# Hybrid decoder layer on one core: order of the differential norm, the dilated sum, the gate chunks and the MLP's first products

## The chip, the core and the metric

One NeuronCore of a Trainium2 chip runs the whole layer in one launch. It has five engines with a queue each: TensorE (PE; matmuls and transposes, its weight loads counted as PEld), VectorE (DVE), ScalarE (ACT), GpSimd (POOL) and SyncE (SP), which issues most DMA transfers; ScalarE issues the others. The metric is device time of one execution in microseconds (us), lower is better.

## The reference

Input x is 1024 tokens by 1024 channels, float32. What is computed, cut to what matters here:

```python
h = rms_norm(x, mix_norm_g)
proj = h @ w_in                       # q, k, v of four mixers, gate logits (4 x 1024 wide)
o_a = stick_breaking(...)             # 4 heads of 64
o_b = dilated(...)                    # 3 groups x 4 heads, windows 128/512/2048, dilation 1/4/16
                                      #   out = sum_g softmax_g(lse_g) * out_g
o_c = forgetting(...)                 # 4 heads
o_d = differential(...)               # 4 heads, softmax minus lam * softmax
o_d = rms_norm(o_d, diff_g) * diff_out_scale        # per head, over its 64 channels
branch = einsum('bsnc,ncd->bsnd', [o_a, o_b, o_c, o_d], w_branch)
gates = sigmoid(gate_logit)
x = x + sum_n(gates * branch) @ w_out
h = rms_norm(x, mlp_norm_g)
x = x + square(relu(h @ w_up)) @ w_down             # 4096 wide
return rms_norm(x, final_norm_g)
```

## The kernel before

All products are float32 in three matmuls: each operand is split into a high part (ScalarE or POOL copies it) and a low part (VectorE or POOL subtracts), and `mm3` (lines 150 to 152) adds high x high, high x low and low x high in PSUM. Weights come in pieces of 128x512 through the tags "wr" (raw, from SP), "wh" and "wl" (split), four buffers each.

Nobody writes out the order on each engine. The program is traced in the order of the Python text; a planner then simulates a timeline, takes at each moment the earliest traced instruction of an engine that is ready, and gives out the buffers of a tag as they come free. Lower work is thus pulled forward into gaps that the plan sees. On the chip each engine then runs its list strictly in that order.

Stages:

1. Norm of x and transposition to hTh, hTl (lines 214 to 222).
2. Twelve attention units (lines 831 to 866), two head pairs each of: differential (units 0, 1), dilated group 0 (2, 3), 1 (4, 5), 2 (6, 7), forgetting (8, 9), stick-breaking (10, 11). The loop attends unit i, makes `N_BEFORE[i]` gate chunks, projects unit i+1, makes `N_AFTER[i]` gate chunks. A gate chunk (`gate_ahead`) computes 128 gate logits of one branch for all 1024 tokens, 48 matmuls of 512 columns named lg, and stores them in DRAM (gl). They fill TensorE while attention waits for other engines; 26 of the 32 chunks are made here. `attend_diff` ends with the norm of the differential branch (lines 656 to 678): per half of the tokens, squares, a matmul with a block of ones (rms), logarithm and exponential on ScalarE, a correction step and the product on VectorE. After unit 9 come `dil_weights` and `dil_combine` (lines 732 to 781), which load the three dilated outputs and their weights (dow), multiply on POOL, add on VectorE and store ys. Score rows and norm scratch share the five buffers of tag "s"; q and k tiles the twelve of tag "qk".
3. Gating: for branches 3, 2, 1, 0 and eight column blocks dm, `gate` loads stored logits (sg<-gl) or computes those that are left (pg), `branch` multiplies by w_branch (pb), by the gate on VectorE (line 930), and adds to the merged sum (lines 933, 935) on VectorE or POOL. For the last branch the sum is split into mh and ml (lines 936, 937), the operands of the output projection `out_proj` (po), which adds to x1 (line 979).
4. `norm2` for the eight token blocks t (lines 1034 to 1063): scale (xn, line 1041), transpose (nt), split into the MLP's operands. The MLP's products are made in seven-product (Strassen-Winograd) form; blocks 4 to 7 feed differences called t1, t2, b22, and in place in raw t3 and t4.
5. MLP up: sixteen pairs of 128 columns (`up_pair`, products p1 to p7, matmuls named pu); the first two pairs run together. MLP down with the final norm behind it (pd).

Of the kernel before, what the change touches and what calls it, by code (L numbers as in the profile page):

```python
# [2 lines left out]

# [18 lines left out]
P = 128  # L22
T = 1024
# [19 lines left out]
N_BEFORE = (1, 4, 3, 3, 0, 0, 0, 0, 0, 1, 1, 0)  # L43
N_AFTER = (0, 1, 1, 0, 0, 0, 0, 0, 1, 0, 3, 3)
N_MID = (0, 4)
# [4 lines left out]

DW_AT = 2

UORDER = (0, 1, 2, 3, 4, 5)
# [8 lines left out]
def kernel(  # L62
# [128 lines left out]

    ys_d = [[dram.tile([P, T], F32, name=f"ys_{n}_{p}") for p in range(2)] for n in range(4)]
    dil_d = [[dram.tile([P, T], F32, name=f"dil_{g}_{p}") for p in range(2)] for g in range(3)]
    st_d = [dram.tile([2, 4, T], F32, name=f"st_{g}") for g in range(3)]
# [11 lines left out]
    with ExitStack() as actx:  # L206
# [282 lines left out]
        ahead = [(n, dm) for dm in (0, 2, 4, 6, 1, 3, 5, 7) for n in ORDER_N[1:]]  # L489
        ahead += [(ORDER_N[0], NK - 1), (ORDER_N[0], NK - 2)]  # L490

# [126 lines left out]
        def attend_diff(pr, qs, ks, vt):  # L618
            y = y_tile()
            for h in range(2):  # L620
                bias = ap_.tile([P, T], F32, tag="s", bufs=NS, name=nm("tb"))
                nc.vector.tensor_scalar_mul(bias, dist, DIF_SLOPES[2 * pr + h])
                for th in range(2):
                    o_ps = ps_o.tile([P, 512], F32, tag="o", name=nm("o"))
                    for qt in (2 * th, 2 * th + 1):
# [27 lines left out]
                        causal_pv(o_ps, vt, h, qt, rows)  # L653
                    o_evac(o_ps, y, h, th, 1)

            for th in range(2):
                sl = slice(th * 512, th * 512 + 512)
                sq = s_tile("sq")[:, 0:512]
                sh = ap_.tile([P, 512], F32R, tag="ptile", bufs=NPT, name=nm("sh"))
                slo = ap_.tile([P, 512], F32R, tag="ptile", bufs=NPT, name=nm("slo"))  # L660
                nc.scalar.activation(sq, y[:, sl], AF.Square)
                nc.scalar.copy(sh, sq)
                nc.vector.tensor_sub(slo, sq, sh.bitcast(F32))
                ps = ps_t.tile([P, 512], F32, tag="t", name=nm("rms"))
                nc.tensor.matmul(ps, ones_blk, sh, start=True, stop=False)
                nc.tensor.matmul(ps, ones_blk, slo, start=False, stop=True)
                m_ = s_tile("m_")
                m, r0 = m_[:, 0:512], m_[:, 512:1024]
                nc.scalar.activation(m, ps, AF.Identity, bias=eps_col)
                nc.scalar.activation(r0, m, AF.Ln)  # L670
                nc.scalar.activation(r0, r0, AF.Exp, scale=-0.5)

                nc.vector.tensor_mul(m, m, r0)
                nc.vector.tensor_mul(m, m, r0)
                nc.vector.tensor_scalar(m, m, -0.5, 1.5, op0=ALU.mult, op1=ALU.add)
                nc.vector.tensor_mul(m, m, r0)
                nc.vector.scalar_tensor_tensor(y[:, sl], y[:, sl], dg_col, m, op0=ALU.mult, op1=ALU.mult)
            nc.scalar.dma_start(ys_d[3][pr], y)

# [83 lines left out]
        def dil_combine():  # L763

            for p in range(2):
                for th in range(2):
                    sl = slice(th * 512, th * 512 + 512)
                    acc = None
                    for g in range(3):
                        ow = s_tile("dow")  # L770
                        o, w = ow[:, 0:512], ow[:, 512:1024]
                        nc.sync.dma_start(o, dil_d[g][p][:, sl])
                        for h in range(2):
                            nc.sync.dma_start(w[64 * h:64 * h + 64],
                                              dw_d[g, 2 * p + h:2 * p + h + 1, sl].to_broadcast([64, 512]))
                        nc.gpsimd.tensor_mul(o, o, w)
                        if acc is None:
                            acc = o
                        else:
                            nc.vector.tensor_add(acc, acc, o)  # L780
# [75 lines left out]
        for i in range(len(units)):  # L856
            nxt()
            for _ in range(N_BEFORE[i]):
                gate_ahead(*ahead.pop(0))
            if i + 1 < len(units):  # L860
                nxt = units[i + 1]()
            for _ in range(N_AFTER[i]):
                gate_ahead(*ahead.pop(0))
            if i == max(len(units) - 1 - DW_AT, 2 * max(UORDER.index(g) for g in (1, 2, 3)) + 1):
                dil_weights()
                dil_combine()

# [12 lines left out]
    with tc.tile_pool(name="gate", bufs=1, reuse_waits="tile") as gp:  # L880
# [39 lines left out]
        def branch(n, dm, th, w, ys, sg):  # L920
# [9 lines left out]
            nc.vector.tensor_mul(sg, pb, sg)  # L930
            add = (nc.vector, nc.gpsimd)[dm % 2 if n == ORDER_N[-1] else th].tensor_add
            if n != ORDER_N[-1]:
# [55 lines left out]
        for c in range(3):  # L988
            ws = wcols(w_out, c * 256, 256, nc.vector)
            for b in range(2):  # L990
                out_proj(b, c, ws)
                for dm in [left.pop(0) for _ in range(min(len(left), (2, 1)[b] if c < 2 else 1))]:
                    if dm % 2 == 0:
                        w = w_br(n, dm)
                    branch(n, dm, 1, w, ys, sgs[dm])
        assert not left
        load_x1(1)
# [36 lines left out]
    def norm2(t):  # L1034
# [16 lines left out]
        if t >= NH:  # L1051
# [13 lines left out]

    steps = ((3, (0, 1), nc.vector), (0, (2, 3), nc.vector), (1, (2, 3), nc.vector), (2, (2,), nc.vector),
             (3, (2, 3), nc.vector), (2, (3,), nc.gpsimd))
    for c, bs, eng in steps:
        ws = wcols(w_out, c * 256, 256, eng)
        for b in bs:  # L1070
            out_proj(b, c, ws)
            if (b, c) in ((0, 3), (1, 3), (2, 3), (3, 2)):
                norm2(2 * b)
                norm2(2 * b + 1)


    def load_pair(j):

        res = {}
        for n, k0, c0 in (("a11", 0, 0), ("a12", NH, 0), ("a22", NH, P), ("a21", 0, P)):  # L1080
            src = w_up[k0 * P:(k0 + NH) * P, j * 256 + c0:j * 256 + c0 + P].rearrange("(k p) c -> p k c", p=P)
            if j == 0:
                q = wp.tile([P, 520], F32, tag="wr", bufs=NWR, name=nm("wr"))[:, :H]
            else:
                q = up_[j % 2].tile([P, H], F32, tag="wq", bufs=4, name=nm("wq"))
            nc.sync.dma_start(q.rearrange("p (a b) -> p a b", a=NH), src)
# [7 lines left out]

    q0 = load_pair(0)
    gm_c.close()
    sa_d = {}
    up_c = ctx.enter_context(ExitStack())
    upt = up_c.enter_context(tc.tile_pool(name="upt", bufs=1, reuse_waits="tile"))
    up_ = [None, upt]  # L1100
    q1 = load_pair(1)

    def up_pair(j, q, c1, c2):

        def ctile(n):
            p_ = up_[(c2 if n[0] == "o" else c1)]
            return p_.tile([P, H], F32, tag="c", bufs=8, name=nm(n))

        s1, s2 = (upt.tile([P, H], F32, tag="ws", bufs=4, name=nm("ws")) for _ in range(2))
        pss = {}  # L1110
# [72 lines left out]

    ab = [up_pair(0, q0, 1, 0), up_pair(1, q1, 1, 0)]
    for i in ("s", "p1", "p2", "p6", "p5", "t3", "p7", "p3", "t4", "p4"):
        if i[0] == "t":
            for t in range(NH):
                split(part(i, t), raw[t][:, "34".index(i[1])])
            if i == "t4":
                rw_c.close()  # L1190
                up_[0] = up_c.enter_context(tc.tile_pool(name="up", bufs=1, reuse_waits="tile"))
                q = load_pair(2)
        else:
            for p_ in ab:
                p_[i]()
    for p_ in ab:
        p_["end"]()
    for j in range(2, NPAIR):
# [4 lines left out]
        q = q2  # L1203
    up_c.close()
    h2a_c.close()
    m_ctx.close()
# [160 lines left out]
```

## Time and profile before

| | us |
|---|---|
| median of 3 runs | 1934.98 |
| lowest, highest | 1934.52, 1936.77 |
| the profiled execution's own time | 1935.1 |
| span of its trace | 1933.4 |
| PE busy | 1847.4 |
| DVE busy | 1092.3 |
| ACT busy | 840.0 |
| POOL busy | 798.3 |

The span runs from the first to the last instruction of one profiled execution; rows of the profile give times from its start. Rows by stretch give the length, then for each engine its busy time and number of instructions, the mean clock that TensorE was granted (1.00 is full), the share of the DMA engines that was busy and GB/s. A row by instruction gives line, engine, operation, output and inputs; in a bracket stands the engine's idle time before it and whose result ended that. Where only three durations stand, they are minimum, median and maximum in ns.

### The profile page before, as it was taken

The numbers are of one execution on the slowest core, as the hardware profiler recorded it, in microseconds if no ns is written. First come the engines' busy times: TensorE is split into PE (matmuls) and PEld (weight loads), VectorE is DVE, ScalarE is ACT, GpSimd is POOL, SyncE is SP. The second block draws the span as 40 slices with busy tenths as digits, with TensorE's granted clock in tenths as the row PEclk, the third lists the DMA queues.
The fourth block names the chain that finished last, engine by engine and source line by source line (L and its number), as shares of the span: only waits on it lengthen the run. The fifth ranks groups of instructions, "written<-read, shape, count | busy, mean of one in ns | idle before, by whom it ended". The sixth has DMA issues, their size and how long they took to land.

```text
span 1933.4 us, 27274 instructions
## 1 busy us (share of the span) xinstructions
PE 1847.4 (96%) x9635; PEld 1551.8 (80%) x9635; DVE 1092.3 (56%) x1896; ACT 840.0 (43%) x1723; POOL 798.3 (41%) x727
## 2 busy tenths in 40 slices
PE   7999999999999999999899989969999998999997
PEld 7888877888888889878777779958888887788885
DVE  5143464535444456556761686595444444959587
ACT  4133443445444344424541543544554543444354
POOL 4333244422222433462313562175565631617164
PEclk9999999999999999999999989989999999999999
DMA  4734113234242312272203764434444439665355
GB/s 148 165 92 126 50 49 88 60 88 138 61 143 56 88 56 68 55 214 70 73 18 110 254 200 139 156 109 154 162 146 150 146 109 365 210 187 175 113 175 185
DMA packets 210104, 249.08 MB, mean 129 GB/s; under 512 B 16944, under 2 KB 136112, under 8 KB 209968
## 3 DMA queue, kind: packets, MB, share of 16 engines
q1 hardware_dynamic: 172288, 172.72, 29.6%
q10 hardware_dynamic: 37680, 74.63, 11.6%
q8 instruction: 76, 1.25, 0.3%
q14 instruction: 60, 0.49, 0.1%
HBM read 170.58 MB, written 63.08 MB: 121 GB/s over the span
## 4 chain that ended last, share of the span: by engine, by line
PE 81%; DVE 7%; DMA 5%; POOL 3%; issue 2%; ACT 2%; SPq 0%; POOLq 0%; DVEq 0%; ACTq 0%
PE pu L1127 5%; PE pu L1126 5%; PE pu L1125 5%; PE lg L150 5%; PE lg L151 5%; PE lg L152 5%; PE pd L1269 4%; PE pd L1268 4%; PE lin L152 4%; PE lin L151 4%; PE pd L1267 4%; PE lin L150 4%; PE pt L422 3%; PE linv L151 2%; PE linv L150 2%; PE linv L152 2%
## 5 line engine op out<-in xcount | busy, mean ns | idle before, releaser
L129 POOL TENSOR_SCALAR wh<-wr 128x512 fp32r<-128x512 f32 (+1 forms) x156 | 106.3, 684 | 420.8 <-PE linv L152 144.3
L130 POOL TENSOR_TENSOR wl<-wr,wh 128x512 fp32r<-128x512 f32 (+1 forms) x160 | 223.1, 1399 | 9.1
L1267 PE MATMUL pd<-wh,sh 128*128 128x512 f32 x448 | 175.1, 396 | 5.4 <-ACT sh L1028 5.3
L1268 PE MATMUL pd<-wl,sh 128*128 128x512 f32 x448 | 175.3, 396 | 0.0
L1269 PE MATMUL pd<-wh,sl 128*128 128x512 f32 x448 | 168.1, 397 | 3.5 <-DVE sl L1029 3.5
L150 PE MATMUL lg<-hTh,wh 128*128 128x512 f32 x416 | 165.9, 399 | 2.6 <-ACT gs L486 2.6
L151 PE MATMUL lg<-hTl,wh 128*128 128x512 f32 x416 | 165.6, 398 | 0.0
L152 PE MATMUL lg<-hTh,wl 128*128 128x512 f32 x416 | 165.2, 397 | 0.0
L1029 DVE TENSOR_TENSOR sl<-sr,sh 128x512 fp32r<-128x512 f32 x112 | 111.8, 999 | 85.2 <-ACT sh L1028 85.1
L151 PE MATMUL lin<-hTl,wh 128*128 128x512 f32 x384 | 153.6, 400 | 0.0
L150 PE MATMUL lin<-hTh,wh 128*128 128x512 f32 x384 | 153.2, 399 | 0.0
L152 PE MATMUL lin<-hTh,wl 128*128 128x512 f32 x384 | 152.0, 399 | 0.0
L1028 ACT CAST sh<-sr 128x512 fp32r<-128x512 f32 x112 | 69.6, 622 | 161.6 <-PE pd L1268 139.4
L427 DVE TENSOR_TENSOR ptl<-pt,pth 128x512 fp32r<-128x512 f32 (+2 forms) x168 | 99.6, 605 | 66.8 <-ACT pth L426 65.6
L426 ACT CAST pth<-pt 128x512 fp32r<-128x512 f32 (+2 forms) x168 | 85.3, 524 | 113.4 <-PE pt L422 108.9
L150 PE MATMUL linv<-wh,hTh 128*128 128x256 f32 (+1 forms) x384 | 112.4, 295 | 1.8 <-POOL wh L129 1.7
L151 PE MATMUL linv<-wl,hTh 128*128 128x256 f32 (+1 forms) x384 | 112.0, 292 | 0.0
L152 PE MATMUL linv<-wh,hTl 128*128 128x256 f32 (+1 forms) x384 | 111.5, 291 | 0.0
L1267 PEld LDWEIGHTS pd<-wh,sh 128*128 128x128 f32 x448 | 84.3, 188 | 27.1 <-ACT sh L1028 7.1
L1269 PEld LDWEIGHTS pd<-wh,sl 128*128 128x128 f32 x448 | 84.5, 189 | 25.8 <-DVE sl L1029 6.4
L1268 PEld LDWEIGHTS pd<-wl,sh 128*128 128x128 f32 x448 | 84.5, 189 | 20.1 <-DVE wl L1029 0.2
L431 PE MATMUL o<-pth,v 128*128 128x256 f32 (+1 forms) x348 | 92.0, 276 | 8.9 <-DVE y L442 4.2
(349 smaller groups left out, 5110.4 us busy)
## 6 DMA issues: line engine op xcount, KB each, us to landing
wr<-in_w_in_dram SPq DMA_DIRECT2D x132, 256.0 KB
br<-in_w_down_dram SPq DMA_DIRECT2D x96, 256.0 KB
sr<-sa_s SPq DMA_DIRECT2D x64, 256.0 KB
wq<-in_w_up_dram SPq DMA_DIRECT2D x60, 256.0 KB
gl<-gs ACTq DMA_DIRECT2D x52, 256.0 KB
sg<-gl SPq DMA_DIRECT2D x52, 256.0 KB
sa_s<-o ACTq DMA_DIRECT2D x48, 256.0 KB
sr<-sa_a SPq DMA_DIRECT2D x48, 256.0 KB
```

The source lines that it names most:

```text
L129: nc.gpsimd.tensor_scalar(hi, raw, 1.0, 1.0, op0=ALU.mult, op1=ALU.mult)
L130: (eng or nc.gpsimd).tensor_sub(lo, raw, hi.bitcast(F32))
L150: nc.tensor.matmul(ps, ah, bh, start=(i == 0), stop=False, skip_group_check=True)
L151: nc.tensor.matmul(ps, ah, bl, start=False, stop=False, skip_group_check=True)
L152: nc.tensor.matmul(ps, al, bh, start=False, stop=(i == n - 1), skip_group_check=True)
L427: nc.vector.tensor_sub(lo[:, :n], ps[:, :n], hi[:, :n].bitcast(F32))
L1029: nc.vector.tensor_sub(o[1], i, o[0].bitcast(F32))
L1125: nc.tensor.matmul(ps, w_, bh[:, k], start=start and k == 0, stop=False, skip_group_check=True)
L1126: nc.tensor.matmul(ps, w_, bl[:, k], start=False, stop=False, skip_group_check=True)
L1267: nc.tensor.matmul(ps, sh[0][:, ts_], w[0], start=start and j == 0, stop=False, skip_group_check=True)
L1268: nc.tensor.matmul(ps, sh[0][:, ts_], w[1], start=False, stop=False, skip_group_check=True)
L1269: nc.tensor.matmul(ps, sh[1][:, ts_], w[0], start=False, stop=last and j == NPAIR - 1, skip_group_check=True)
```

## The change

Five edits:

- The differential norm leaves `attend_diff`. The raw output is stored in DRAM (yd), and a new `diff_norm(pr)` loads it back by halves, with its scratch in two tiles of tag "s", and stores each half. It is called after the projection that follows units 3 and 4.
- `dil_combine` moves from unit 9 to unit 11, behind its attention and ahead of the last gate chunks; its tiles take tag "qk" in place of "s". `dil_weights` stays.
- The last entry of `N_AFTER` goes from 3 to 6, so 29 chunks are made ahead and three are left for the gating stage.
- In the last branch all additions are on VectorE, and for each output product the branch products of the second half come ahead of it, the w_out pieces behind them.
- `norm2(6)` and `norm2(7)` move behind the first product p1 of the MLP's pairs 0 and 1; pair 0's weights load after `norm2(3)`. The buffers of the first two and of all odd pairs are slices of x1's memory in place of a pool of their own.

```diff
-N_AFTER = (0, 1, 1, 0, 0, 0, 0, 0, 1, 0, 3, 3)
+N_AFTER = (0, 1, 1, 0, 0, 0, 0, 0, 1, 0, 3, 6)
+NORM_AT = 3
...
-        ahead += [(ORDER_N[0], NK - 1), (ORDER_N[0], NK - 2)]
+        ahead += [(ORDER_N[0], dm) for dm in range(NK - 1, 2, -1)]
...
+            nc.scalar.dma_start(yd_d[pr], y)
+
+        def diff_norm(pr):
             for th in range(2):
                 sl = slice(th * 512, th * 512 + 512)
-                sq = s_tile("sq")[:, 0:512]
+                ysq, mr = s_tile("ysq"), s_tile("mr")
+                y, sq, m, r0 = ysq[:, 0:512], ysq[:, 512:1024], mr[:, 0:512], mr[:, 512:1024]
...
-                nc.scalar.activation(sq, y[:, sl], AF.Square)
+                nc.sync.dma_start(y, yd_d[pr][:, sl])
+                nc.scalar.activation(sq, y, AF.Square)
...
-            nc.scalar.dma_start(ys_d[3][pr], y)
+                nc.scalar.dma_start(ys_d[3][pr][:, sl], y)
...
-                        ow = s_tile("dow")
+                        ow = ap_.tile([P, T], F32, tag="qk", bufs=NQK, name=nm("dow"))
...
             if i + 1 < len(units):
                 nxt = units[i + 1]()
+            if i == len(units) - 1:
+                dil_combine()
             for _ in range(N_AFTER[i]):
                 gate_ahead(*ahead.pop(0))
+            if i in (NORM_AT, NORM_AT + 1):
+                diff_norm(i - NORM_AT)
             if i == max(len(units) - 1 - DW_AT, 2 * max(UORDER.index(g) for g in (1, 2, 3)) + 1):
                 dil_weights()
-                dil_combine()
...
-            add = (nc.vector, nc.gpsimd)[dm % 2 if n == ORDER_N[-1] else th].tensor_add
+            add = (nc.vector, nc.gpsimd)[0 if n == ORDER_N[-1] else th].tensor_add
...
         for c in range(3):
-            ws = wcols(w_out, c * 256, 256, nc.vector)
             for b in range(2):
-                out_proj(b, c, ws)
-                for dm in [left.pop(0) for _ in range(min(len(left), (2, 1)[b] if c < 2 else 1))]:
+                for dm in [left.pop(0) for _ in range(min(len(left), 1 if b else 2))]:
                     if dm % 2 == 0:
                         w = w_br(n, dm)
                     branch(n, dm, 1, w, ys, sgs[dm])
+                if b == 0:
+                    ws = wcols(w_out, c * 256, 256, nc.vector)
+                out_proj(b, c, ws)
...
-            if j == 0:
+            if j == 1:
                 q = wp.tile([P, 520], F32, tag="wr", bufs=NWR, name=nm("wr"))[:, :H]
+            elif j == 0 or j % 2:
+                q = next(slot_q)
             else:
-                q = up_[j % 2].tile([P, H], F32, tag="wq", bufs=4, name=nm("wq"))
+                q = up_.tile([P, H], F32, tag="wq", bufs=4, name=nm("wq"))
...
+    slots = [[s[:, i * H:(i + 1) * H] for i in range(8)] for s in sums_x1]
+    slot_q, slot_c, slot_s = cycle(slots[0][:4]), cycle(slots[0][4:] + slots[1][4:]), cycle(slots[1][:4])
...
     for c, bs, eng in steps:
         ws = wcols(w_out, c * 256, 256, eng)
         for b in bs:
             out_proj(b, c, ws)
-            if (b, c) in ((0, 3), (1, 3), (2, 3), (3, 2)):
+            if (b, c) in ((0, 3), (1, 3), (2, 3)):
                 norm2(2 * b)
                 norm2(2 * b + 1)
+                if b == 1:
+                    q0 = load_pair(0)
...
-            for p_ in ab:
+            for k, p_ in enumerate(ab):
                 p_[i]()
+                if i == "p1":
+                    norm2(NT - 2 + k)
```

More of the change, by code (lines that the diff above doesn't have):

```diff
@@ L2 @@
 from contextlib import ExitStack
+from itertools import cycle
 import numpy as np
@@ L192 @@
     ys_d = [[dram.tile([P, T], F32, name=f"ys_{n}_{p}") for p in range(2)] for n in range(4)]
+    yd_d = [dram.tile([P, T], F32, name=f"yd_{p}") for p in range(2)]
     dil_d = [[dram.tile([P, T], F32, name=f"dil_{g}_{p}") for p in range(2)] for g in range(3)]
@@ L666, in attend_diff @@
                 nc.tensor.matmul(ps, ones_blk, slo, start=False, stop=True)
-                m_ = s_tile("m_")
-                m, r0 = m_[:, 0:512], m_[:, 512:1024]
                 nc.scalar.activation(m, ps, AF.Identity, bias=eps_col)
@@ L676, in attend_diff @@
                 nc.vector.tensor_mul(m, m, r0)
-                nc.vector.scalar_tensor_tensor(y[:, sl], y[:, sl], dg_col, m, op0=ALU.mult, op1=ALU.mult)
-            nc.scalar.dma_start(ys_d[3][pr], y)
+                nc.vector.scalar_tensor_tensor(y, y, dg_col, m, op0=ALU.mult, op1=ALU.mult)
+                nc.scalar.dma_start(ys_d[3][pr][:, sl], y)
         def attend_dil(g, pr, q, k, kl, vt, mnl):
@@ L1063, in norm2 @@
             nc.gpsimd.tensor_sub(b21, b21, t2)
[L1066 to L1071, printed above, removed]
-            if (b, c) in ((0, 3), (1, 3), (2, 3), (3, 2)):
-                norm2(2 * b)
-                norm2(2 * b + 1)
     def load_pair(j):
@@ L1093, in wsplit @@
         return o
-    q0 = load_pair(0)
-    gm_c.close()
     sa_d = {}
[L1098 to L1101, printed above, removed]
+    slots = [[s[:, i * H:(i + 1) * H] for i in range(8)] for s in sums_x1]
+    slot_q, slot_c, slot_s = cycle(slots[0][:4]), cycle(slots[0][4:] + slots[1][4:]), cycle(slots[1][:4])
     def up_pair(j, q, c1, c2):
         def ctile(n):
-            p_ = up_[(c2 if n[0] == "o" else c1)]
-            return p_.tile([P, H], F32, tag="c", bufs=8, name=nm(n))
-        s1, s2 = (upt.tile([P, H], F32, tag="ws", bufs=4, name=nm("ws")) for _ in range(2))
+            if c2 if n[0] == "o" else c1:
+                return next(slot_c)
+            return up_.tile([P, H], F32, tag="c", bufs=8, name=nm(n))
+        s1, s2 = next(slot_s), next(slot_s)
         pss = {}
@@ L1181, in up_pair @@
         return {"s": sums, "p1": p1, "p6": p6, "p2": p2, "p5": p5, "p7": p7, "p3": p3, "p4": p4, "end": end}
-    ab = [up_pair(0, q0, 1, 0), up_pair(1, q1, 1, 0)]
+    steps = ((3, (0, 1), nc.vector), (0, (2, 3), nc.vector), (1, (2, 3), nc.vector), (2, (2,), nc.vector),
+             (3, (2, 3), nc.vector), (2, (3,), nc.gpsimd))
+    for c, bs, eng in steps:
+        ws = wcols(w_out, c * 256, 256, eng)
+        for b in bs:
+            out_proj(b, c, ws)
+            if (b, c) in ((0, 3), (1, 3), (2, 3)):
+                norm2(2 * b)
+                norm2(2 * b + 1)
+                if b == 1:
+                    q0 = load_pair(0)
+    ab = [up_pair(0, q0, 1, 0), up_pair(1, load_pair(1), 1, 0)]
     for i in ("s", "p1", "p2", "p6", "p5", "t3", "p7", "p3", "t4", "p4"):
@@ L1190 @@
                 rw_c.close()
-                up_[0] = up_c.enter_context(tc.tile_pool(name="up", bufs=1, reuse_waits="tile"))
+                up_c = ctx.enter_context(ExitStack())
+                up_ = up_c.enter_context(tc.tile_pool(name="up", bufs=1, reuse_waits="tile"))
                 q = load_pair(2)
         else:
-            for p_ in ab:
+            for k, p_ in enumerate(ab):
                 p_[i]()
+                if i == "p1":
+                    norm2(NT - 2 + k)
     for p_ in ab:
@@ L1204 @@
     up_c.close()
+    gm_c.close()
     h2a_c.close()
```

## The prediction

> **What bounds the kernel now.** I read the page's first part, then TensorE's list of waits, then the busy time of each engine in stretches cut at the stages that the change touches, then single instructions in time order.
>
> ```profile
> span 1933.4 us, 27274 instructions
> PE 1847.4 (96%) x9635; PEld 1551.8 (80%) x9635; DVE 1092.3 (56%) x1896; ACT 840.0 (43%) x1723; POOL 798.3 (41%) x727
> ```
>
> TensorE is busy for 96%. The change removes no matmul, so all it can win is in the 86.0 us in which TensorE has nothing (1933.4 - 1847.4), and in stretches at half clock.
>
> ```profile
> PE nt L1046 <- DVE xn L1041: 6.9, 4, 4.4
> PE po L152 <- DVE ml L937: 5.0, 2, 2.5
> PE sc L637 <- DVE mn L638: 4.4, 1, 4.4
> PE pu L1127 <- DVE wl L1029: 4.0, 2, 2.5
> PE rms L665 <- ACT sh L662: 1.2, 1, 1.2
> PE po L151 <- DVE wl L130: 0.5, 1, 0.5
> PE rms L666 <- DVE slo L663: 0.4, 1, 0.4
> ```
>
> Total, number and longest in us: many causes, none large; VectorE (DVE) ends most of them.
>
> ```profile
> core 0: us, PE busy (x) PEld busy (x) DVE busy (x) ACT busy (x) POOL busy (x), PEclk, DMA share, GB/s
> 225.00:258.00 33.00, 25.88 (x152) 22.46 (x151) 20.85 (x37) 17.38 (x32) 11.98 (x10) 0.90 0.15 41
> 398.00:430.00 32.00, 31.77 (x199) 28.17 (x199) 12.46 (x29) 17.67 (x32) 7.91 (x8) 1.00 0.31 88
> 430.00:475.00 45.00, 42.40 (x322) 39.24 (x320) 26.96 (x86) 27.56 (x83) 7.45 (x8) 1.00 0.31 97
> 855.00:876.00 21.00, 15.91 (x75) 11.74 (x73) 11.95 (x14) 7.89 (x17) 11.38 (x15) 1.00 0.74 196
> 876.00:945.00 69.00, 69.00 (x378) 57.75 (x378) 44.65 (x49) 31.98 (x69) 14.23 (x25) 1.00 0.17 54
> 945.00:990.00 45.00, 34.52 (x209) 28.02 (x209) 40.42 (x46) 29.92 (x65) 15.04 (x21) 0.96 0.18 53
> 1025.00:1075.00 50.00, 50.00 (x217) 40.40 (x216) 6.74 (x10) 5.58 (x10) 18.59 (x20) 1.00 0.25 73
> 1075.00:1110.00 35.00, 34.63 (x148) 27.41 (x147) 28.36 (x36) 22.31 (x38) 22.42 (x19) 1.00 0.93 319
> 1110.00:1148.00 38.00, 34.87 (x158) 27.77 (x157) 37.48 (x46) 19.76 (x34) 30.07 (x22) 1.00 0.70 223
> 1148.00:1164.00 16.00, 11.96 (x70) 11.66 (x71) 7.50 (x11) 2.88 (x7) 2.74 (x3) 0.68 0.29 102
> 1254.00:1300.00 46.00, 30.25 (x144) 23.50 (x143) 43.70 (x45) 21.45 (x43) 37.61 (x24) 0.81 0.38 121
> 1300.00:1590.00 290.00, 290.00 (x1251) 234.74 (x1250) 141.37 (x182) 144.82 (x238) 160.06 (x115) 1.00 0.43 144
> ```
>
> The idle of TensorE (length minus PE busy) sits in five places: 7.1 us at the first differential norm, 5.1 at the dilated sum, 10.5 where the gate chunks run out beside the last attention unit, 4.0 at the first output products, 15.8 at the last norms before the MLP. Where fillers are there (876 to 945, 1300 to 1590) it is 0. A 512-wide matmul costs 290/1251 = 0.232 us.
>
> **Part A, differential norm.** It leaves the end of attend_diff and comes after the projections of units 4 and 5, through DRAM: two 512 KB stores of y, four 256 KB loads on SP, four 256 KB stores instead of two of 512 KB. Arithmetic, matmuls and table loads are the same.
>
> ```profile
> 251.12 0.39 PE L637 MATMUL sc<-dm,dm 128*128 128x256 f32 x1 [4.38 <-DVE mn L638]
> L661 ACT ACTIVATE sq<-y x4: 616/618/620, 224.7 to 413.0; 128x512 f32<-128x512 f32 x4
> L670 ACT ACT_TABLE_LOAD  x4: 1283/1283/1283, 239.4 to 419.6; - x4
> L674 DVE TENSOR_TENSOR m__344_1425<-m__344_1425 x1: 1671/1671/1671, 244.7 to 244.7; 128x512 f32<-128x512 f32 x1
> ```
>
> At the first norm TensorE waits 1.2 + 0.4 for the rms operands, then 4.4 for unit 1's scores, whose L638 is queued on VectorE behind the norm's multiplies (L674 took 1.67). These 6.0 go. The clock is 0.90 over 33 us, 3.3 us lost; I count half as following the 4.4 wait: 1.7. Saved: 7.7. The second norm lies in 398 to 430, where TensorE idles only 0.2: nothing to win there.
>
> The new place: a half of a norm costs ScalarE five operations of 0.62 and two table loads of 1.28, 5.7 us, so 11.4 per norm on ScalarE, in a dilated stretch like 430 to 475, where it has 27.6 of 45 busy and TensorE already idles 2.6. Queued behind the norm there are L710's exponentials and the ptile casts, for which the transposes and P·V wait; the cover is the next unit's lin and linv matmuls. Bounds per norm: 0.2 (the second norm) to 7.7 (the first). The second is the nearer row, as fillers stand beside it; I take 2.1. A saves 7.7 - 4.2 = **3.5** (ends -7.7 and 7.3). The extra 2 MB find a DMA share of 0.31, and ten issues more on SP and ScalarE at about 0.4 each stand beside other work: nothing, unless SP waits for a slot of tag "s" with weights queued behind; that is inside the upper bound.
>
> **Part B, dilated sum out of 855 to 876.**
>
> ```profile
> 864.52 0.44 PE L403 MATMUL sc<-kA,qA 128*128 128x384 f32 x1 [2.99 <-ACT sg L513]
> 867.63 0.44 PE L422 MATMUL pt<-ident,sg 128*128 128x128 f32 x2 [1.22 <-DVE sg L517]
> L774 SPq DMA_DIRECT2D dow<-dw x24: 444/502/1113, 830.6 to 860.0; - x24
> L776 POOL TENSOR_TENSOR dow<-dow x12: 1263/1292/1751, 834.4 to 865.2; 128x512 f32<-128x512 f32 x12
> L780 DVE TENSOR_TENSOR dow<-dow,dow x8: 671/1267/1766, 838.3 to 867.5; 128x512 f32<-128x512 f32 x8
>   DMA dow<-dw: 14.1, 6
> ```
>
> The sg tiles of the stick-breaking unit share tag "s" with dow here. With dow in tag "qk" the waits of 2.99 and 1.22 go: **4.2** (0 to 5.1). Late next is the unit's own chain of VectorE scans.
>
> **Part C, three more chunks and the sum beside the last unit.** Three chunks are 3 x 48 x 0.232 = 33.4 us of matmuls, moved from 1025-1075 into the stretch that idles 10.5 us. There TensorE was 100% busy on them, so the gating stage gets shorter by 33.4 and the last unit longer by 33.4 - 10.5. With the clock (0.96 over 45 us, 1.7) that saves 12.2. Each chunk takes along two weight loads on SP, two splits on POOL, two ScalarE copies, two stores and two loads; a chunk already hidden in 876 to 945 shows the price, 0.
>
> Against it: the sum now stands there, before the six chunks in the program. Its 12 multiplies are 15.5 us of POOL, which also waits up to 14.1 for dow's transfers, and the kp memsets and weight splits queue behind them; its 24 issues of dw alone hold SP for 24 x 0.50 = 12.0 us with wr loads behind; its 8 adds are 10.1 us of VectorE, busy 40.4 of 45. TensorE still has 33.4 - 10.5 = 22.9 us of filler to cover the delay. Bounds: 0, to the 5.1 that the same sum cost at 855; I take half, 2.5. C saves **9.7** (7.1 to 12.2).
>
> **Part D, output products.**
>
> ```profile
> L930 DVE TENSOR_TENSOR sg<-pb,sg x48: 675/678/692, 1089.6 to 1200.2; 128x512 f32<-128x512 f32 x48
> L935 DVE TENSOR_TENSOR sg<-mg,sg x8: 676/686/693, 1137.7 to 1199.6; 128x512 f32<-128x512 f32 x8
> L935 POOL TENSOR_TENSOR sg<-mg,sg x8: 1585/1660/1674, 1138.0 to 1200.9; 128x512 f32<-128x512 f32 x8
> 1149.58 0.54 PE L152 MATMUL po<-wh,ml 128*128 128x256 f32 x1 [2.52 <-DVE ml L937]
> 1153.66 0.58 PE L152 MATMUL po<-wh,ml 128*128 128x256 f32 x1 [2.47 <-DVE ml L937]
> ```
>
> The first product waits twice for ml, at the end of the chain DVE L930, POOL L935, ACT mh, DVE ml. The change makes eight adds 0.69 on VectorE instead of 1.66 on POOL (VectorE +5.5 us, outside the saturated 1110-1148 for the most part) and puts two branch products, 2 x 12 x 0.232 = 5.6 us, ahead of the out_proj. The 5.0 go. In 1148-1164 the clock is 0.68, 5.1 us lost, 3.9 of it with work on TensorE (half of one 2.5 us wait taken off): also gone. New: w_out's splits now come after the branches' VectorE work, so po may wait for wl; between the 0.5 that stands in the list of waits and all 8.9 of the gain. I take 3.0, nearer to the row: **5.9** (0 to 8.4).
>
> The Trainium skill, TensorE: Matmul & The Clock Gate, section HAM oscillation, holds that the clock halves after idle gaps of more than about 3.4 us. By that rule the waits of 2.5 don't cause the slow stretch, D is 2.0 and the time 1911; the trace differs, since 2.52 is the longest gap ahead of it.
>
> **Part E, norms and MLP.** p1 of both first pairs now comes before norm2(6) and norm2(7), and pair 0's weights load earlier, into x1's old place.
>
> ```profile
> 1264.73 0.40 PE L1125 MATMUL pu<-b11h,wh 128*128 128x512 f32 x1
> 1286.39 0.80 PE L1127 MATMUL pu<-b11h,wl 128*128 128x512 f32 x1 [2.46 <-DVE wl L1029]
> 1294.83 0.50 PE L1126 MATMUL pu<-mh,wh 128*128 128x512 f32 x1 [1.86 <-DVE mh L1029]
> ```
>
> VectorE is the bound here: 43.7 of 46 us. The planner has already pulled pair 0's p1 to 1264.7; what can still move into the idle is pair 1's p1 and both p2, so that at 1294.8, when the last norm's t2 operand is ready, one product less remains: 12 x 0.232 = 2.8. Pair 0's three POOL sums can start earlier, which may take POOL's interference off a few VectorE operations; I take 1.7 for that and the clock. E saves **4.5** (0, as VectorE has the same work, to 8, half of the 15.8 idle).
>
> **Sum.** 3.5 + 4.2 + 9.7 + 5.9 + 4.5 = 27.8. The profiled execution took 1935.1 us with a span of 1933.4; the median shown is 1934.98, the same within 0.2. 1935.1 - 27.8 = 1907.3, so 1907 us.
>
> **Rivals.**
> - *Everything fills:* upper ends, 7.3 + 5.1 + 12.2 + 8.4 + 8 = 41: 1894 us. For it: idle 0 wherever fillers stand. Against: VectorE at 43.7 of 46.
> - *The stalls move along:* both norms cost 7.7 again and the sum 5.1: A -7.7, C 7.1, total 14.0, 1921 us. For it: ScalarE at 27.6 of 45 before the norm comes.
> - *VectorE holds D and E:* these give 0; 17.4, 1918 us. For it: 37.5 of 38 us in 1110-1148.
> - *Slower: the gating stage doesn't shrink.* If transfers and VectorE set its length, the 33.4 us are added beside attention and not taken off in 1025-1148: C is 9.7 - 33.4 = -23.7, total -5.6, 1941 us. It turns to slower once more than 27.8 of the 33.4 stay. For it: DMA share 0.93 and VectorE 37.5 of 38. Against: over these 123 us VectorE has 72.6, transfers 71.7, and TensorE would still have 119.5 - 33.4 = 86.1.
>
> **How the numbers follow.** Forecast (1899 to 1916) 0.46; everything fills 0.13; stalls move along 0.14; VectorE holds D and E 0.10; parts cancel to within 0.2% 0.08; slower 0.09. 0.2% (3.9 us) is about what a measurement can tell from no change here. Faster: 0.46 + 0.13 + 0.14 + 0.10 = 0.83. Range 1890 to 1931: it leaves out the slower rival, most of the cancelling and a little of the low end.
>
> **What the next profile would show.** A: no wait of 4 us for L638 near 250, no rms wait above 2 us beside the dilated units. B: no wait of sc for sg L513 near 865. C: lg until the end of the last unit, no idle row like 945-990, three pg chunks instead of six. D: no po wait for ml, clock 1.00 there. E: both p1 before the last eight transposes, less than 15 us idle, VectorE still above 90%. Wrong if POOL or SP, waiting for dow, starves the chunks, or if the planner, which orders all of this anew, opens waits in places that the change doesn't touch.

## The result and the profile after

The changed kernel takes 1905.97 us (median of 6 runs, 1904.28 to 1908.19) against 1936.03 us for the kernel before on the same chip (6 runs, 1934.52 to 1939.13): ratio 0.9843, 95% interval 0.9831 to 0.9856. The forecast was 1907 us. The profiled execution took 1908.19 us, the longest of the six, with a span of 1906.4.

The first part of the page of the changed kernel:

```profile
span 1906.4 us, 27323 instructions
PE 1840.0 (97%) x9635; PEld 1551.8 (81%) x9635; DVE 1089.6 (57%) x1904; ACT 847.3 (44%) x1731; POOL 789.8 (41%) x719
```

The span is 27.0 us shorter. TensorE has the same 9635 matmuls; its idle time fell from 86.0 to 66.4 us (1906.4 - 1840.0), which is 19.6, and its busy time by 7.4. The clock doesn't explain the latter: inside the stretches at half clock between 150 and 1650 us TensorE was busy for 33.9 us before and 36.4 us after. What does is not shown.

TensorE's list of waits in the changed kernel (total, number, longest in us):

```profile
PE nt L1057 <- DVE xn L1052: 5.9, 3, 3.2
PE rms L674 <- ACT sh L671: 5.8, 1, 5.8
PE po L155 <- DVE ml L947: 2.7, 2, 1.4
PE po L154 <- POOL wl L133: 2.7, 3, 1.7
PE pt L426 <- ACT s L717: 2.4, 1, 2.4
PE pu L1127 <- DVE wl L1040: 0.6, 1, 0.6
PE po L154 <- DVE wl L133: 0.6, 1, 0.6
```

The 4.4 for L638, the 4.0 of pu for wl (0.6 is left) and 2.3 of the 5.0 for ml are gone. The wait of rms for sh was 1.2 and is 5.8, and that of po for wl from POOL, 1.0 before, is 2.7.

Busy time by stretch in the changed kernel, in the columns of the rows before:

```profile
225.00:258.00 33.00, 30.88 (x191) 27.27 (x190) 18.91 (x53) 13.64 (x37) 15.36 (x17) 0.95 0.18 49
258.00:510.00 252.00, 251.84 (x1423) 217.79 (x1422) 121.01 (x307) 113.08 (x256) 86.42 (x88) 1.00 0.32 92
465.00:510.00 45.00, 45.00 (x253) 38.87 (x252) 22.49 (x56) 26.42 (x56) 13.86 (x14) 1.00 0.40 109
510.00:545.00 35.00, 25.48 (x169) 22.76 (x168) 19.09 (x53) 22.71 (x52) 0.00 (x0) 0.80 0.10 38
855.00:876.00 21.00, 21.00 (x120) 17.63 (x119) 13.54 (x17) 8.53 (x19) 8.91 (x9) 1.00 0.65 199
870.00:892.00 22.00, 17.13 (x77) 13.82 (x76) 11.68 (x13) 7.56 (x17) 15.28 (x13) 0.84 0.71 212
990.00:1048.00 58.00, 58.00 (x275) 47.70 (x274) 16.45 (x19) 13.43 (x25) 20.11 (x19) 1.00 0.40 128
1048.00:1092.00 44.00, 44.00 (x190) 35.51 (x189) 30.59 (x43) 26.22 (x45) 28.19 (x24) 1.00 0.91 310
1230.00:1275.00 45.00, 33.60 (x163) 26.22 (x162) 44.62 (x48) 23.97 (x47) 40.56 (x27) 0.85 0.35 115
```

The row for 258 to 510 reads as follows before the change:

```profile
258.00:510.00 252.00, 246.29 (x1342) 208.90 (x1341) 119.11 (x311) 108.81 (x248) 86.64 (x91) 1.00 0.29 83
```

The old idle at 855 to 876 and at the end of the last unit is filled, that at 225 to 258 fell from 7.1 to 2.1 us, and 5.7 us in small pieces between 258 and 510 fell to 0.2. The idle of 9.5 us in 510 to 545 and of 4.9 us in 870 to 892 is new. Before the MLP VectorE has 44.62 of 45 us and TensorE still lacks 11.4.

To place the saving I cut both traces at four events that both have: the first matmul of cum_ps in the forgetting units, the 288th matmul with w_branch (pb), the 720th of the output projection (po), the first of MLP down (pd). Length of each stage in us, with the leave-one-out kernels told of below:

| | to cum_ps | to 288th pb | to 720th po | to pd | rest |
|---|---|---|---|---|---|
| before | 656.2 | 476.2 | 121.9 | 347.0 | 332.1 |
| after | 653.3 | 460.5 | 117.4 | 342.5 | 332.7 |
| norm back (A undone) | 656.9 | 460.4 | 116.7 | 342.7 | 332.4 |
| sum back (B undone) | 652.1 | 465.9 | 117.5 | 342.9 | 333.0 |
| 3 chunks (C undone) | 650.4 | 472.8 | 116.8 | 343.1 | 332.2 |
| products as before (D undone) | 651.8 | 460.5 | 120.6 | 342.0 | 332.5 |
| norms and MLP as before (E undone) | 652.0 | 459.6 | 117.5 | 347.0 | 330.5 |

Each part moves the stage that it stands in; B and C share the second. There is one trace for each kernel. A stage that no edit touches repeats to within about 3 us in the first and last column and 1 us in the third and fourth, which is finer than the runs' times can tell. The 653.3 of the changed kernel is at the upper end of what its first stage takes with the norm as changed (650.4 to 653.5).

### The profile page after: what moved, and what is told of

Same layout as the page of the kernel before. It is cut to its first block, busy times and chain, and to the rows that moved or that the text cites. A ratio compares the mean times of both kernels' runs of the same rounds, so it can differ in the third digit from the quotient of the medians.

```text
span 1906.4 us, 27323 instructions
## 1 busy us (share of the span) xinstructions
PE 1840.0 (97%) x9635; PEld 1551.8 (81%) x9635; DVE 1089.6 (57%) x1904; ACT 847.3 (44%) x1731; POOL 789.8 (41%) x719
## 3 DMA queue, kind: packets, MB, share of 16 engines
q10 hardware_dynamic: 39120, 77.25, 12.2%
## 4 chain that ended last, share of the span: by engine, by line
PE 85%; DVE 5%; DMA 4%; POOL 2%; issue 1%; ACT 1%; SPq 0%; POOLq 0%; DVEq 0%; ACTq 0%
PE pu L1126 5%; PE pu L1127 5%; PE pu L1125 5%; PE lg L153 5%; PE lg L154 5%; PE lg L155 5%; PE lin L154 5%; PE lin L153 5%; PE lin L155 5%; PE pd L1286 4%; PE pd L1285 4%; PE pd L1284 4%; PE pt L426 3%; PE linv L153 2%; PE linv L154 2%; PE linv L155 2%
## 5 line engine op out<-in xcount | busy, mean ns | idle before, releaser
L154 PE MATMUL lg<-hTl,wh 128*128 128x512 f32 x464 | 185.9, 401 | 0.0
L153 PE MATMUL lg<-hTh,wh 128*128 128x512 f32 x464 | 185.3, 399 | 0.0
L155 PE MATMUL lg<-hTh,wl 128*128 128x512 f32 x464 | 185.0, 399 | 0.0
L153 PEld LDWEIGHTS lg<-hTh,wh 128*128 128x128 f32 x464 | 87.8, 189 | 17.6
L155 PEld LDWEIGHTS lg<-hTh,wl 128*128 128x128 f32 x464 | 87.8, 189 | 17.4
```

The lines of the kernel that those rows point to most:

```text
L153: nc.tensor.matmul(ps, ah, bh, start=(i == 0), stop=False, skip_group_check=True)
L154: nc.tensor.matmul(ps, ah, bl, start=False, stop=False, skip_group_check=True)
L155: nc.tensor.matmul(ps, al, bh, start=False, stop=(i == n - 1), skip_group_check=True)
```

## Experiments

Each diff is against the changed kernel. Its ratio is to the kernel before, run on the same chip.

**Each part undone alone.** Norm: `attend_diff` ends with the norm of before, and

```diff
-            if i in (NORM_AT, NORM_AT + 1):
-                diff_norm(i - NORM_AT)
```

> The changed kernel with the differential norm back at the end of attend_diff. Theory (each part fills its own gap, and the norm's new place costs a stall of its own near 530): about 3 us slower than the changed kernel, 1909 us; the 4.4 us wait for L638 near 250 comes back, the waits of 5.8 and 2.4 us near 530 go. Rival (the new stall eats the whole gain): within 1 us of the changed kernel, 1906. Second rival (forecast's size of 7.7 for the first norm, with a cheap new place): 1913.

Measured: 1910.70 us, 0.9865 (0.9848 to 0.9881). Some 4 us more than after by the ratios, in the first stage (3.6, with the spread of 3 just told). TensorE's waits at 230 to 260 us with the norm back:

```profile
PE sc L640 <- DVE mn L641: 4.4, 1, 4.4
PE rms L668 <- ACT sh L665: 1.2, 1, 1.2
```

They are the two of before to the tenth, so the first norm's waits were read rightly.

Sum:

```diff
-            if i == len(units) - 1:
-                dil_combine()
...
                 dil_weights()
+                dil_combine()
...
-                        ow = ap_.tile([P, T], F32, tag="qk", bufs=NQK, name=nm("dow"))
+                        ow = s_tile("dow")
```

> The changed kernel with the dilated sum back behind unit 9 and its tiles back in tag s. Theory of the forecast (sg tiles wait for slots of tag s that dow holds): 4 to 5 us slower, 1911, with a wait of sc for sg L517 near 860. Rival (the stall comes with the sum wherever it stands, since its store ys<-dow waits in ScalarE's queue for the addition, and it only moved from 864 to 883): within 1.5 us of the changed kernel, 1906.

Measured: 1912.82 us, 0.9875 (0.9860 to 0.9889); 5.4 us more in the second stage. The wait of sc for sg is back at 859.75 us with 2.38. ScalarE's list of waits from 850 to 880 us tells what sg waited for:

```profile
ACT sg L517 <- DMA ys<-dow: 2.2, 1, 2.2
```

Chunks:

```diff
-N_AFTER = (0, 1, 1, 0, 0, 0, 0, 0, 1, 0, 3, 6)
+N_AFTER = (0, 1, 1, 0, 0, 0, 0, 0, 1, 0, 3, 3)
...
-        ahead += [(ORDER_N[0], dm) for dm in range(NK - 1, 2, -1)]
+        ahead += [(ORDER_N[0], dm) for dm in range(NK - 1, NK - 3, -1)]
```

> The changed kernel with three chunks beside the last unit instead of six (26 ahead, six left for the gating stage). Theory (the chunks fill TensorE's idle time at the end of attention): 10 to 12 us slower, 1917, with some 10 us idle before the last scores. Rival (the sum, now standing there, already changes the end of attention, and the rest of B and C is not the chunks): less than 5 us slower, 1910.

Measured: 1918.75 us, 0.9903 (0.9887 to 0.9920); 12.3 us more in the second stage, the largest single part. The end of the last unit, with three chunks:

```profile
945.00:990.00 45.00, 38.79 (x205) 31.99 (x204) 31.44 (x34) 20.61 (x44) 13.46 (x16) 0.89 0.18 53
```

6.2 us of idle and a clock of 0.89 return there.

Output products: the loop and the alternating additions of before.

```diff
-            add = (nc.vector, nc.gpsimd)[0 if n == ORDER_N[-1] else th].tensor_add
+            add = (nc.vector, nc.gpsimd)[dm % 2 if n == ORDER_N[-1] else th].tensor_add
...
+            ws = wcols(w_out, c * 256, 256, nc.vector)
             for b in range(2):
-                for dm in [left.pop(0) for _ in range(min(len(left), 1 if b else 2))]:
+                out_proj(b, c, ws)
+                for dm in [left.pop(0) for _ in range(min(len(left), (2, 1)[b] if c < 2 else 1))]:
```

> The changed kernel with the order of branch and output products and the alternating additions of before. Theory (the shorter chain and one branch product more ahead of po take about half of the waits for ml): 2.7 us slower, 1908.7, two po waits of 2.5 us come back. Forecast's size: 5.9 us slower, 1912.

Measured: 1909.08 us, 0.9853 (0.9834 to 0.9873); by the times alone not told from the changed kernel, but its third stage is 3.2 us longer, and two waits of 2.5 and 2.7 us for ml are back (1125 to 1145 us):

```profile
PE po L155 <- DVE ml L947: 5.2, 2, 2.7
```

Norms and MLP: the order of steps, `norm2` calls and buffers of before.

```diff
-                if i == "p1":
-                    norm2(NT - 2 + k)
```

> The changed kernel with norm2(6), norm2(7) ahead of the MLP and the buffers of before. Theory (products that need no late norm fill TensorE while VectorE works through the norms): 6 us slower, 1912; idle of about 15 us in the stretch from the last out_proj to the p6 products instead of about 11. Rival (VectorE is the bound there and has the same work): within 1.5 us, 1906.

Measured: 1910.00 us, 0.9863 (0.9846 to 0.9879); the fourth stage is 347.0 us, as before. TensorE's waits from 1230 to 1275 us:

```profile
PE nt L1057 <- DVE xn L1052: 6.7, 3, 4.5
PE pu L1138 <- DVE wl L1040: 4.1, 2, 2.5
PE pu L1136 <- ACT wh L1039: 2.0, 1, 2.0
```

The waits of the MLP's first products return. In this kernel, as before the change, 12 matmuls of pu come ahead of the last sixteen transposes nt; in the changed one 48 do.

**The additions alone.** The branch additions alternate again, the new order of products stays (the first pair of lines of the diff for the output products).

> The last branch's additions alternate between VectorE and POOL again; the order of branch products and output products stays as changed. Theory (the order is what counts, since ml is made on VectorE and the change puts two branch products between the making of ml and its reading): within 1 us of the changed kernel, 1905 to 1908 us, and waits for ml of 1.4 us or less each. Rival (the additions on VectorE are what shortened ml's way: POOL takes 1.2 us or more for an addition that VectorE does faster): waits for ml of 2 us or more return and with them the 1.9 us that both halves are worth, 1908 to 1911 us.

Measured: 1911.10 us, 0.9864 (0.9851 to 0.9878); third stage 120.8 us, as long as with the whole part undone (120.6). TensorE's waits from 1125 to 1145 us:

```profile
PE po L155 <- DVE ml L947: 3.5, 3, 2.1
PE po L153 <- ACT mh L946: 0.8, 1, 0.8
```

So the theory falls and the rival holds: with the new order, what part D wins comes from the additions on VectorE; the new order alone wins nothing. The additions with the old order were not run.

**The dilated sum: tiles, queues, engines.** First only the tag: the sum at unit 9 again, its tiles still in "qk".

```diff
-            if i == len(units) - 1:
-                dil_combine()
...
                 dil_weights()
+                dil_combine()
```

> The changed kernel with the dilated sum back behind unit 9, but its tiles left in tag qk. Tells tag from place. Theory of the forecast (slots of tag s are what held up sg): like the changed kernel or a little faster, 1906, no sg wait near 860. Rival (ScalarE's queue, with the store ys<-dow in it): a stall of 4 to 5 us remains, as with the sum wholly back. If q and k tiles of unit 11 wait for the sum's tiles: slower still, 1912.

Measured: 1921.39 us, 0.9918 (0.9902 to 0.9935); the slowest of all. The second stage takes 472.9 us against 465.9 with tag "s" at the same place. TensorE's waits from 835 to 880 us:

```profile
PE pt L426 <- DVE sg L521: 7.7, 3, 4.2
PE o L437 <- DVE ptl L431: 3.2, 2, 2.0
```

Taking the sum out of the slots of tag "s" at the old place makes it worse. That does not clear the slots. No sg waits for a store of dow any more, but the planner now starts the stick-breaking rows (first kp on ScalarE) at 821.1 us, where it starts them at 856.5 us with the sum in tag "s". The sum at 829 to 872 us then stands among these rows, and ScalarE waits behind one of its stores:

```profile
ACT otmp L443 <- DVE dow L787: 10.5, 1, 10.5
```

One hold went and another, larger one came.

In the changed kernel the sum runs from 857 to 909 us and stalls unit 10 instead. The list of waits from 878 to 912 us, and below it two rows of TensorE in time order:

```profile
DVE dow L787 <- POOL dow L783: 7.7, 3, 3.7
ACT sg L517 <- DVE dow L787: 6.3, 1, 6.3
DVE dow L787 <- DMA dow<-dw: 2.4, 1, 2.4
```

```profile
883.20 0.39 PE L437 MATMUL o<-ptl,v 128*128 128x256 f32 x1 [3.17 <-DVE ptl L431]
885.93 0.90 PE L426 MATMUL pt<-ident,sg 128*128 128x128 f32 x3 [1.70 <-DVE sg L521]
```

ScalarE waits 6.3 us for an addition of the sum although its next sigmoid (sg) doesn't need it: the store of ys stands ahead of it in ScalarE's list. So the store was moved to SP's queue.

```diff
-                    nc.scalar.dma_start(ys_d[1][p][:, sl], acc)
+                    nc.sync.dma_start(ys_d[1][p][:, sl], acc)
```

> The changed kernel with one line changed: the store ys<-dow of the dilated sum is issued by SP instead of ScalarE. Theory (ScalarE stands 4 to 6 us behind that store, 6.3 for sg L517 and 4.8 for pth L430, and TensorE's waits of 3.2 and 1.7 near 883 follow from it): 4 to 7 us faster, 1901. Rival (the stall is the sum's hold on VectorE and POOL, or SP's weight loads are now held instead): same, 1906, or slower.

Measured: 1908.57 us, 0.9851 (0.9831 to 0.9871): no gain. ScalarE's wait, from 878 to 912 us, is now on VectorE:

```profile
ACT sg L517 <- DVE sg L521: 10.6, 2, 6.3
```

There additions of the sum stand in front and wait for POOL and the transfers. Then the additions went to POOL as well.

```diff
-                            nc.vector.tensor_add(acc, acc, o)
+                            nc.gpsimd.tensor_add(acc, acc, o)
```

> The dilated sum's two additions go from VectorE to POOL and its store from ScalarE's queue to SP's, so that neither VectorE nor ScalarE has an instruction in its order that waits for the sum's loads; place and tiles as in the changed kernel. Theory (the stall at 880 to 910 us is the order of VectorE and ScalarE behind the sum: 3.17, 1.70 and 1.22 us of idle TensorE and 6.8 us of records at half clock, 3.4 us lost): the waits at 883 and 910 go, 4 to 8 us less than the changed kernel, 1898 to 1902 us. Rival 1 (POOL is held in place of the other two: its weight splits and score memsets stand behind the sum, and TensorE waits for wh, wl or s): 1904 to 1908 us. Rival 2 (the loads of the sum on SP hold the unit's own loads, whatever engine adds): the idle steps at 883 stay with the same releasers, 1904 to 1908 us; told from rival 1 by the releaser.

Measured: 1905.12 us, 0.9834 (0.9821 to 0.9848): not told from the changed kernel. Waits from 878 to 912 us:

```profile
POOL dow L783 <- DMA dow<-dw: 9.6, 3, 4.9
DVE sg L521 <- POOL kp L507: 5.9, 2, 4.7
PE pt L426 <- DVE sg L521: 3.5, 2, 1.9
```

POOL waits for the sum's transfers, with the stick-breaking unit's memset of kp behind. Rival 1 holds in the main (the memset is what TensorE ends up waiting for): whichever of the three engines has the sum in its list waits there for dow<-dw and holds the unit.

**The second norm.** Idle at 510 to 545 us is where `diff_norm(1)` landed. ScalarE in the changed kernel in time order, and TensorE's rows that wait for it:

```profile
524.83 0.69 ACT L676 ACTIVATE mr<-rms,eps_col 128x512 f32<-128x512 f32 x1 [2.84 <-PE rms L675]
525.53 1.28 ACT L677 ACT_TABLE_LOAD   x1
...
527.47 1.28 ACT L678 ACT_TABLE_LOAD   x1
...
529.95 0.62 ACT L671 CAST sh<-ysq 128x512 fp32r<-128x512 f32 x1
```

```profile
530.61 0.80 PE L674 MATMUL rms<-sh,ones_blk 128*128 128x512 f32 x1 [5.83 <-ACT sh L671]
...
537.30 0.69 PE L426 MATMUL pt<-ident,s 128*128 128x128 f32 x2 [2.39 <-ACT s L717]
```

The second half's squares and their copy sh come behind the first half's two table loads, and TensorE, without a filler here, waits 5.83 and then 2.39 us; from 528.9 us on the clock is at half for 13.7 us. One kernel wrote both halves' squares ahead of either logarithm:

```diff
             for th in range(2):
...
+                hs.append((sl, y, m, r0))
+            for sl, y, m, r0 in hs:
                 nc.scalar.activation(r0, m, AF.Ln)
+            for sl, y, m, r0 in hs:
                 nc.scalar.activation(r0, r0, AF.Exp, scale=-0.5)
```

> The changed kernel with diff_norm regrouped: squares and rms matmuls of both halves first, then both logarithms, both exponentials, both correction steps. Same operations, half the changes of table. Theory (TensorE waits 5.8 us near 530 for the second half's squares, which stand on ScalarE behind the first half's two table loads of 1.28): 6 to 9 us faster, 1898, with the half clock there gone. Rival (ScalarE is just too full in the dilated unit): a wait of similar size elsewhere in that unit, 1905.

Measured: 1907.08 us, 0.9842 (0.9823 to 0.9862): the same. The planner put ScalarE's list back in nearly the old order (second square at 529.66 us), so this tested nothing about the chip. Another moved the norm:

```diff
-            if i in (NORM_AT, NORM_AT + 1):
-                diff_norm(i - NORM_AT)
+            if i in (3, 8):
+                diff_norm((3, 8).index(i))
```

> The second differential norm is called behind unit 8's projections (beside the second forgetting unit) and no longer behind unit 4's; the first stays. Theory (what the second norm costs at 530 us is its place: ScalarE reaches its squares behind two table loads and the first half's logarithm and exponential, and no filler stands there, so that TensorE waits 5.83 us for sh and 2.39 us for s, with 13.7 us of records at half clock behind): both waits go, and since TensorE has no idle step over 0.5 us between 550 and 880 us in the changed kernel, none comes back: 8.2 us of waits and up to 6.9 us of clock less, 1893 to 1900 us. Rival 1 (the wait belongs to the norm wherever it runs without a filler unit's slack: one norm is free, the other is not): a wait for sh of 4 us or more appears beside unit 9, 1903 to 1908 us. Rival 2 (the two table loads do more harm beside the forgetting unit, whose ScalarE is busier): 1909 to 1915 us.

Measured: 1908.51 us, 0.9852 (0.9839 to 0.9865): no gain, but not for want of one where the norm left. The first stage is 638.5 us, 14.8 shorter; the second is 476.9, 16.4 longer. Two stretches of the changed kernel (from cum_ps to the first stick-breaking row, and from there to the last row's start), and below them the same two of this one:

```profile
653.30:820.50 167.20, 167.20 (x996) 144.38 (x994) 97.11 (x240) 70.80 (x146) 68.91 (x79) 1.00 0.24 66
820.50:986.30 165.80, 159.18 (x853) 132.50 (x852) 112.15 (x138) 77.63 (x163) 69.71 (x84) 0.98 0.34 104
```

```profile
638.50:836.60 198.10, 196.26 (x1115) 166.28 (x1114) 116.02 (x258) 86.72 (x168) 82.73 (x91) 1.00 0.25 69
836.60:1003.50 166.90, 157.19 (x826) 130.25 (x824) 106.44 (x133) 75.82 (x163) 66.97 (x77) 0.96 0.37 111
```

The planner drew 29 us more of TensorE's work (196.26 - 167.20) ahead of the stick-breaking rows: 93 more lin products and 23 more lg in that stretch. The stick-breaking stretch then starts 16 us later, takes the same 166 to 167 us at a lower clock (0.96 for 0.98), and has 9.7 us of idle where 6.6 stood; 1.8 more come beside unit 9. None of the expectation's three cases: the waits for sh and s went and none of their size came beside unit 9, but the fillers were used up early and missing at the end.

**All together.** Norm behind unit 8, additions and store of the sum on POOL and SP, and all 32 chunks ahead:

```diff
-N_AFTER = (0, 1, 1, 0, 0, 0, 0, 0, 1, 0, 3, 6)
+N_AFTER = (0, 1, 1, 0, 0, 0, 0, 0, 1, 0, 3, 9)
...
-        ahead += [(ORDER_N[0], dm) for dm in range(NK - 1, 2, -1)]
+        ahead += [(ORDER_N[0], dm) for dm in range(NK - 1, -1, -1)]
```

> Three edits on the changed kernel: the second norm behind unit 8's projections, the dilated sum's additions on POOL and its store on SP's queue, and all 32 gate chunks ahead (the nine of the last stage in place of six). Theory (moving the norm alone put the forgetting unit 15 us ahead, 643.8 against 658.6 us, and lost it behind: gate chunks were drawn forward, their last product came at 988.9 in place of 1010.2 us, and 10.0 us of waits with 13.7 us of records at half clock stand between 903 and 1006 us, where no filler was left): with 3 more chunks the last chunk ends at 1010 to 1020 us, most of those waits go, and the time is 7 to 13 us under the changed kernel's, 1893 to 1899 us. Rival 1 (those waits are the sum's and the stick-breaking units' own chain, which no filler reaches): waits of 8 us or more stay between 900 and 1006 us, 1903 to 1908 us. Rival 2 (the waits go, but the three chunks are missed where they were made before, beside the last branch's gates and products at 1010 to 1100 us): no idle step over 1.5 us before 1006 us, new ones behind it, 1900 to 1906 us.

Measured: 1909.70 us, 0.9855 (0.9839 to 0.9872). First stage 639.6, second 477.7. From TensorE's list of waits, and ScalarE's rows in time order:

```profile
PE pb L153 <- ACT yh L904: 9.7, 1, 9.7
```

```profile
1035.80 0.33 ACTq L491 DMA_DIRECT2D gl<-gs  x1
...
1043.59 1.28 ACT L922 ACTIVATE sg<-sg 128x512 f32<-128x512 f32 x2 [6.78 <-DMA sg<-gl]
1044.98 1.97 ACT L904 CAST yh<-yr 128x512 fp32r<-128x512 f32 x3
```

The waits at 990 to 1006 us go, as the theory says, though four steps of 1.2 to 2.2 us stay between 900 and 941; and 9.7 us come behind them, as rival 2 says, if not at its time. The last logits leave for DRAM at 1035.80 us (their chunk, made last, belongs to the branch that is gated first), and ScalarE waits 6.78 us for stored logits to come back. The operand yh, the first of the products with w_branch, stands behind that in ScalarE's list, but it isn't the logits that hold it longest. Its own loads (yr) are issued behind the logits' loads, as SP's rows show:

```profile
1038.98 1.25 SPq L917 DMA_DIRECT2D sg<-gl  x2
1040.32 2.10 SPq L893 DMA_DIRECT2D yr<-ys  x4
```

The sigmoids are done at 1044.87 us, the first yr lands at 1044.96 by its semaphore, and yh starts at 1044.98. No run changed the order of these loads. With the three chunks left for the gating stage there is work of TensorE's own (pg, 1011 to 1047 us) over these loads.

No kernel tried is faster than the changed one beyond the interval.

## Why the prediction was right, point by point

The forecast saving of 27.8 us compares with 27.0 in the spans of the two profiled executions and with 30.1 in the medians (1936.03 - 1905.97). It lies that close in part by luck, with errors of both signs inside it:

| part | forecast | stage of the trace | undone alone, its stage |
|---|---|---|---|
| A | 3.5 | 2.9 | 3.6 |
| B + C | 4.2 + 9.7 = 13.9 | 15.7 | 5.4 and 12.3 |
| D | 5.9 | 4.5 | 3.2 |
| E | 4.5 | 4.5 | 4.5 |
| rest | 0 | -0.6 | |

The terms for the clock (1.7 in A, 1.7 in C, 3.9 in D, part of 1.7 in E) were counted as saved. Where they were counted, stretches at half clock did go or shrink, but new ones opened at 528.9 us (13.7) and 883.9 us (6.8), and over the whole run nothing was won (33.9 us of matmuls inside them before, 36.4 after).

**A: the total near by luck, the terms of the new place wrong.** The first norm's price went much as worked out (back_norm brings its waits back): 225 to 258 us has 5.0 us less idle, for a forecast of 6.0, and a clock of 0.95 for 0.90, which is the 1.7. In the new place each norm was put at 2.1, between 0.2 and 7.7. The first costs nothing that the rows show (465 to 510: TensorE 45.00 of 45). The second costs 8.2 us of waits and a clock of 0.80 over 35 us; taken away from there, its stage loses 14.8 us. That is outside the bound of 7.7: the bound came from a norm with projections beside it, and here TensorE had only attention. What made up for it the prediction didn't count: the 5.7 us of idle between 258 and 510 that went to 0.2. Idle time alone thus gives 1 us of A's 2.9; the other 1.9 is busy time of TensorE, whose cause is open. The forecast for the next profile, no rms wait above 2 us, failed (5.83). The Trainium skill, ScalarE: Activation LUTs, section What ACT_TABLE_LOAD costs, gives about 1283 ns for a table load; the trace agrees (1.28), and two of them stand in this wait.

**B: size near, the hold named rightly, the cure only in part.** The kernel before has this row of ScalarE behind the wait of 2.99:

```profile
864.19 0.28 ACT L513 ACTIVATE sg<-sc 128x128 f32<-128x128 f32 x1 [3.24 <-DMA ys<-dow]
```

This sg reads scores, not ys: it waits until a store out of a dow tile has landed, and the two share the slots of tag "s". So the attribution to the slots stands for this wait, and back_sum shows it again (2.2). It is not the only hold. With the sum in tag "qk" the order of the lists is one: an engine whose list has an instruction of the sum waits there for its loads or additions (sum_tag, sum_sp, sum_pool). With this tag the new place is 12.4 us better in the second stage (460.5 against 472.9); the sum in tag "s" at the new place was not run, so tag and place aren't told apart fully. The stall also didn't go: 3.17 + 1.70 us stand at 883 to 886, twice the 2.5 that the working for C had set aside for it.

**C: right, a little low.** 12.3 us when undone, at the upper end of 7.1 to 12.2. Undone alone, B and C give 17.7 us, together 15.7, so they are not independent. The gating stage did shrink, so the slower rival is out: three pg chunks end at 1047 us, TensorE has 58.00 of 58 us in 990 to 1048 and 44.00 of 44 in 1048 to 1092, with a DMA share of 0.91 in the latter.

**D: mis-sized.** Waits of po for ml fell from 5.0 to 2.7, not to 0, and those for wl are 0.6, not 3.0. The half clock there shrank from 10.2 us, with 7.8 us of matmuls in it, to 3.4, with 3.4, which gives half of 4.4, or 2.2, in place of 3.9. With 2.3 less waiting for ml that is the 4.5 of the stage. The working gave the new order a cover of 5.6 us from two branch products; such a product is two halves of y by three matmuls, 6 and not 12, so two are 2.8 us. The order alone wins nothing (adds_pool); what D wins hangs on the additions, which the working counted only as 0.69 for 1.66. By the rule of the Trainium skill, TensorE: Matmul & The Clock Gate, section HAM oscillation, that the clock halves after idle gaps of more than about 3.4 us, D was 2.0. The trace differs again: the clock falls to half at 1136.5 us, for 3.4 us, where the longest gaps ahead are 1.29 and 1.43 us.

**E: right in the mechanism, to the tenth by luck.** 4.5 us, and VectorE is the bound, with 44.62 of 45. Three products of 12 matmuls moved ahead of the last transposes, as worked out (12 matmuls before, 48 after). The waits of pu for wl fell from 4.0 to 0.6 and those of nt for xn stayed (6.9 to 5.9). But the 1.7 put down for the clock and POOL isn't seen as clock: the stretch at half clock there has 9.2 us of matmuls before and 9.0 after. TensorE's idle time in this stage fell by 4.3 us, more than the 2.8 of one product.

**The rivals.** *Everything fills* and *the stalls move along* were each half true: the sum's stall moved by 20 us, the second norm's was new, the others were filled. *VectorE holds D and E* fell: these gave 9.0 together by the stages, 7.7 when undone alone.

## What to carry to other kernels

Cut both traces at events that both have and compare stage by stage: parts that the times could barely tell apart (3 to 12 us of 1906) show at once in the stage that they stand in. A stall that an idle row shows is not yet a gain, since behind it the next chain may set the end: the 14.8 us won by moving the second norm were lost again in the next stage (16.4), where fillers ran out beside the attention's own chain, or loads from DRAM came next. And when an instruction waits for a result that it doesn't read, it is held by a slot or by what stands ahead of it in its engine's list. Here the dilated sum held the unit in both ways: freeing the slots alone (sum_tag) brought out the other hold, and moving the sum's instructions to another engine moved the wait with them.

## What the runs showed of the hardware

- Half-clock stretches came in steps: 3.4, 6.8, 10.2, 13.7 and 17.1 us. The 13.7 us at 528.9 go on while TensorE works between the waits of 5.83 and 2.39 us, and one began at 1136.5 with no idle gap above 1.43 us in the 8 us ahead of it.
- Between 150 and 1650 us they came to 44.4 us before and 47.8 after, with 33.9 and 36.4 us of matmuls in them.
- With all chunks ahead, 7.8 us lay between the issue of the last logits' store (1035.80 us) and the sigmoid on logits loaded back (1043.59), at a DMA share of 0.77 in between.
